# RWKV-7's running sums as TensorE products, and the experts' tokens and results as rows in DRAM placed by indirect transfers

## The chip, the cores and the metric

The kernel runs on one core of a Trainium2 chip. Such a core has TensorE (PE, matrix products), VectorE (DVE), ScalarE (ACT), GpSimd (POOL) and SyncE (SP, which here only issues transfers), each with a queue of its own that it works off in order, and 16 DMA engines. The metric is the device time of one execution in microseconds (us); lower is better.

## What is computed

The kernel computes two layers of a denoiser's backbone for 256 latent tokens and 256 context tokens of 1024 features, all in float32. Layer 0 is a bidirectional Mamba-2 mixer and a dense SwiGLU. Layer 1 is a bidirectional RWKV-7 mixer (called mixer 2 here, the second) and eight SwiGLU experts of 3584, of which each latent token uses two. The change touches layer 1:

```python
def _rwkv_features(u, ...):            # per direction d
    logw.append(_heads(-RW_DECAY_SCALE * jax.nn.sigmoid((w0[d] + jnp.tanh(xw @ w1[d]) @ w2[d]).astype(f32))))
    a = jax.nn.sigmoid((a0[d] + (xa @ a1[d]) @ a2[d]).astype(f32))
...
def _rwkv_scan(r, logw, k, v, kk, a, s0, need_y):
    ...
        sa = jnp.einsum('bhvk,bhk->bhv', S, kk_t)
        S = S * w_t[:, :, None, :] - sa[..., None] * b_t[:, :, None, :] + v_t[..., None] * k_t[:, :, None, :]
...
def _moe(u, router_w, w_in, w_out):
    logits = (u @ router_w).astype(jnp.float32)
    top_v, top_i = lax.top_k(logits, TOP_K)
    wts = jax.nn.softmax(top_v, axis=-1)
    gates = jnp.einsum('btk,btke->bte', wts, jax.nn.one_hot(top_i, N_EXPERTS, dtype=jnp.float32)).astype(u.dtype)
    for e in range(N_EXPERTS):
        out = out + gates[..., e:e + 1] * _swiglu(u, w_in[e], w_out[e])
```

## The kernel before

Every product with a weight matrix is made in three products of rounded float32 (`fp32r`): the operands are split in a high part (ACT's cast) and the rest (DVE's difference), and `mm3` adds hi·hi, hi·lo and lo·hi in PSUM (lines 212 to 214).

**Order.** The program is written as generators that `weave` interleaves; a scheduler then places each engine's instructions by a simulated timeline, and the engines work them off in that order. Buffers come from pools; a tile that takes over a buffer waits for the last use of the one before.

**Mixer 2** (924 to 1592 us of the profiled execution). The recurrence is worked in chunks of 64 tokens. Four units (context or latent tokens, first or second half of the heads) go through `stage`, once per direction. A direction of a unit has two pairs of chunks. `lora` makes, for a pair, the low-rank products and their sigmoids as Tanh: for each of four blocks of 128 features one product for the decay (L1013) and one for the rate (L1014), and a Tanh of 128x128 for each (L1015, L1017), with the bias `w0h` in the instruction; POOL adds 1 to the decays (`th`, L1023). `decays` runs once per chunk: a scan along the tokens on DVE (L1043, with `smask` zero where a block begins) gives the running sum `cum`, and ACT makes exp(−c·cum) (`Dp`, L1047), its last column (`dc`, L1049) and exp(c·cum) (L1050). `operands` scales by these, and `grams` makes the chunk's products (L1082, L1091). Between these run the inversions, the scans over chunks and the features of the other half, woven in.

**Experts** (1640 to 2641 us). Tokens lie in 128 slots per expert. `route(e)` makes one-hot matrices for a pair of experts (`one_hot`: DVE compares, PE transposes and a gate product) and `gather` multiplies the normalised tokens `uhi`/`ulo` by them (L1733, 32 products per pair), then scales, adds the modulation and splits into `xg`. `expert` goes over 28 tiles of the first matrix and 14 of the second, of 1 MB each, loaded by SP in that order (L1581) into 10 raw buffers; each is cast and differenced in two pieces (L1719, L1720, three buffers each) and used in 12 products. Seven times per expert the product of gate and value (L1754, L1756) is transposed (L1759) into `HT`. For each half of the output, DVE multiplies the result by gate and modulation (L1782), ACT and DVE split it (L1783, L1784), four products with the transposed one-hot send it back to its tokens (L1787, L1788), and DVE adds these to the residual (L1790). In experts 1, 3 and 5 `between` runs `route` for the next pair. Two lines set this:

```python
            nxt = (lambda: route(e + 1)) if e % 2 and e < 7 else None
            R = expert(so, PT[:, e % 2, :], gs[:, e % 2:e % 2 + 1], nxt, e == 7) or R
```

## Time and profile before

| what | before |
|---|---|
| median of three runs | 2652.65 us (2651.37 to 2655.88) |
| the profiled execution | 2658.37 us, its span 2656.5 us |
| mean granted clock of PE | 0.931 |
| PE, DVE, ACT, POOL busy | 92%, 77%, 55%, 13% of the span |
| layer 0: mixer, output product, dense SwiGLU | 0 to 924 us |
| mixer 2 | 924 to 1592 us |
| its end, routing | 1592 to 1640 us |
| the eight experts | 1640 to 2641 us |
| tail: final norm and output | to 2656.5 us |

The page's parts are averages over the span; the stages have different limits, so they are read stage by stage: the 40 slices for where a stage begins and ends, then the waits and the busy time in a stretch, then single lines. A wait is told as "engine, tile and line <- what ended it". The granted clock is that of PE, as a share of full speed (2.4 GHz; 0.5 is the lower of its two levels).

### The profile page before, as it was taken

To read this page: it belongs to the slowest core of one execution; us is meant where nothing else is said; L and a number is where in the kernel's file an instruction comes from. 1 tells how busy PE (TensorE), PEld (TensorE's weight loads), DVE (VectorE), ACT (ScalarE), POOL (GpSimd) and SP (SyncE) were. 2 spreads that over 40 slices of the span, in tenths; PEclk is the share of its full clock that TensorE was granted. 3 is DMA by queue.
4 is the path that set the end of the run, shared out by engine and by line. 5 is a ranking of instruction groups with operands and counts; after the bars stand their busy time and mean duration, and the time that the engine had idled before them with its cause. 6 is when DMAs were issued, how large, how long until landed. Compare 5 with 4: busy or idle time off the path is not lost. (4 is left out here: it accounts for less than half of the span.)

```text
span 2656.5 us, 44879 instructions
## 1 busy us (share of the span) xinstructions
PE 2440.9 (92%) x17770; PEld 1994.8 (75%) x17770; DVE 2039.1 (77%) x3070; ACT 1457.5 (55%) x2322; POOL 341.9 (13%) x434
## 2 busy tenths in 40 slices
PE   7999998999999978679868797999999999999997
PEld 4777776878888767568767686887888788878875
DVE  5787888667554377687676645999999899989997
ACT  4454545333223265435335225877787777778775
POOL 1011102000000254233432211000000000000001
PEclk9999999999999978577888687999999999999999
DMA  7323232336564221022020116899999899989994
GB/s 260 120 88 102 74 104 80 122 121 201 169 203 140 85 94 48 16 68 80 18 73 2 59 39 265 318 359 341 359 370 358 327 363 368 357 320 368 367 340 158
DMA packets 99211, 511.63 MB, mean 193 GB/s; under 512 B 11648, under 2 KB 19072, under 8 KB 55216
## 3 DMA queue, kind: packets, MB, share of 16 engines
q1 hardware_dynamic: 97520, 506.52, 52.8%
q8 instruction: 141, 2.31, 0.4%
q10 hardware_dynamic: 1472, 2.16, 0.3%
q14 instruction: 78, 0.64, 0.1%
HBM read 506.54 MB, written 2.10 MB: 191 GB/s over the span
## 5 line engine op out<-in xcount | busy, mean ns | idle before, releaser
L1720 DVE TENSOR_TENSOR wlo<-wraw,whi 128x1024 fp32r<-128x1024 f32 x662 | 798.4, 1224 | 69.6 <-ACT whi L1719 49.1
L1719 ACT CAST whi<-wraw 128x1024 fp32r<-128x1024 f32 x662 | 694.3, 1051 | 207.1 <-PE gu L214 111.9
L213 PE MATMUL gu<-wlo,xg 128*128 128x512 f32 x896 | 355.3, 397 | 1.5 <-DVE wlo L1720 0.7
L214 PE MATMUL gu<-whi,xg 128*128 128x512 f32 x896 | 349.8, 391 | 0.0
L212 PE MATMUL gu<-whi,xg 128*128 128x512 f32 x896 | 336.4, 392 | 1.1 <-ACT xg L1739 0.9
L206 ACT CAST whi<-wraw 128x1024 fp32r<-128x1024 f32 (+2 forms) x126 | 129.7, 1030 | 218.4 <-PE acc L213 206.2
L207 DVE TENSOR_TENSOR wlo<-wraw,whi 128x1024 fp32r<-128x1024 f32 (+2 forms) x126 | 151.8, 1205 | 110.0 <-ACT whi L206 109.8
L213 PEld LDWEIGHTS gu<-wlo,xg 128*128 128x128 f32 x896 | 168.5, 188 | 42.3 <-DVE wlo L1720 6.1
L212 PEld LDWEIGHTS gu<-whi,xg 128*128 128x128 f32 x896 | 168.4, 188 | 38.1 <-ACT xg L1739 1.6
L214 PEld LDWEIGHTS gu<-whi,xg 128*128 128x128 f32 x896 | 168.7, 188 | 31.5
L213 PE MATMUL y<-wlo,HT 128*128 128x512 f32 x448 | 178.4, 398 | 2.3 <-DVE wlo L1720 2.0
L212 PE MATMUL y<-whi,HT 128*128 128x512 f32 x448 | 176.6, 396 | 3.0 <-DVE xg L1740 3.0
L214 PE MATMUL y<-whi,HT 128*128 128x512 f32 x448 | 176.1, 393 | 0.0
L212 PE MATMUL acc<-h2hi,whi 128*128 128x512 f32 x352 | 137.4, 393 | 3.4 <-ACT h2hi L343 3.4
L1794 POOL TENSOR_TENSOR wraw<-yx,SH 128x512 f32<-128x512 f32 x4 | 7.5, 1875 | 1022.1 <-DVE yx L1790 1022.1
L213 PE MATMUL acc<-h2lo,whi 128*128 128x512 f32 x352 | 137.4, 391 | 0.0
L212 PE MATMUL acc<-hhi,whi 128*128 128x512 f32 (+1 forms) x328 | 135.8, 414 | 0.8 <-ACT whi L206 0.8
L214 PE MATMUL acc<-h2hi,wlo 128*128 128x512 f32 x352 | 134.7, 391 | 0.3 <-DVE wlo L207 0.3
L213 PE MATMUL acc<-hlo,whi 128*128 128x512 f32 (+1 forms) x328 | 134.1, 409 | 0.0
L214 PE MATMUL acc<-hhi,wlo 128*128 128x512 f32 (+1 forms) x328 | 133.6, 408 | 0.0
L305 POOL TENSOR_TENSOR sqa<-sqa,sq 128x512 f32<-128x512 f32 (+1 forms) x35 | 47.5, 1357 | 579.2 <-issue 311.3
L260 DVE SCALAR_TENSOR_TENSOR wraw<-wraw,scb 128x1024 f32<-128x1024 f32 x56 | 68.5, 1223 | 50.2 <-DMA wraw<-in_w_modT_dram 49.4
(565 smaller groups left out, 5358.5 us busy)
## 6 DMA issues: line engine op xcount, KB each, us to landing
wraw<-in_w_mi_dram SPq DMA_DIRECT2D x219, 1024.0 KB, 5.0
wraw<-in_w_mo_dram SPq DMA_DIRECT2D x112, 1024.0 KB, 5.0
wraw<-in_w_modT_dram SPq DMA_DIRECT2D x56, 512.0 KB, 3.9
wraw<-in_w_ffi_dram SPq DMA_DIRECT2D x44, 512.0 KB, 3.6
wraw<-in_w_mod_dram SPq DMA_DIRECT2D x40, 512.0 KB, 5.0
wraw<-in_w_mb_dram SPq DMA_DIRECT2D x40, 512.0 KB, 4.8
wraw<-in_w_mbo_dram SPq DMA_DIRECT2D x16, 512.0 KB, 4.1
wraw<-in_w_ffo_dram SPq DMA_DIRECT2D x16, 512.0 KB, 3.6
```

Of the source, the lines that this page charges most:

```text
L206: S.copy(hi, raw)
L207: eng[q % len(eng)].tensor_sub(lo, raw, hi.bitcast(F32))
L212: PE.matmul(o, whi, xhi, start=start, stop=False)
L213: PE.matmul(o, whi, xlo, start=False, stop=False)
L214: PE.matmul(o, wlo, xhi, start=False, stop=stop)
L260: V.scalar_tensor_tensor(t, w, 0.5, scb[:, j, :], op0=ALU.mult, op1=ALU.mult, accum_out=mods[l][:, n, j:j + 1])
L305: G.tensor_add(self.acc, self.acc, sq)
L1719: S.copy(hi, raw[:, k:k + 2, :])
L1720: V.tensor_sub(lo, raw[:, k:k + 2, :], hi.bitcast(F32))
L1794: G.tensor_mul(xf[:, tt, 512 * n:512 * n + 512], fs, fg[:, 512 * n:512 * n + 512])
```

## The change

**Mixer 2.** The biases `w0` and `a0` become a 65th row of the low-rank matrices, with a row of ones in the features, so that the Tanh needs no bias of its own: `th` is made with tokens on the partitions in one product of 512 columns and one Tanh, `ta` in four products and one Tanh. `decays` runs once per pair of chunks: four products of 128 columns with a triangular matrix of ones (`tb_f`, `tb_b`) give the running sum in PSUM, and ACT's exponentials read it there for both chunks at once. The second matrix is loaded in two transfers of 65 rows per unit.

**Experts.** Two tensors in DRAM, `XS` and `YS`, hold 128 rows for each expert and 128 more. They are filled with zeros where needed before the dense products of layer 0 (a memset and eight transfers of 0.5 MB on POOL's queue). The first pair is gathered as before. In expert 0 `slots` works out for every token the two rows it belongs to; POOL adds `uhi` and `ulo` and sends each token's row to both (four indirect transfers, 128 rows of 4 KB each). For the experts 2 to 7, SP loads the 128 rows of the expert and PE transposes them, 8 times 128x128, into the same scaling and split. The experts 0 to 6 multiply their result by the modulation alone and store it in `YS` from POOL's queue (14 transfers of 256 KB); in expert 7 `shares` gathers each token's two rows back (four indirect transfers) and DVE adds them with their weights. Expert 7 itself still goes back by its one-hot.

```diff
@@ lora, decays
-            th = tp.tile([128, 2, 4, 64], F32, name=f"th{d}")
+            th = tp.tile([128, 4, 128], F32, name=f"th{d}")
+            p = ms()
+            PE.matmul(p, F["hw"][d][:, ts], l2[0][:65, d], start=True, stop=True)
+            S.activation(flat(th), p, AF.Tanh, scale=0.5)
+            p = ms()
+            for i in range(4):
+                PE.matmul(p[:, 128 * i:128 * i + 128], l2[1][:65, d, 128 * i:128 * i + 128], F["ha"][d][:, ts],
+                          start=True, stop=True)
+            S.activation(flat(ta), p, AF.Tanh, scale=0.5)
             for i in range(4):
-                PE.matmul(p[:, 0:128], l2[:, 0, 128 * i:128 * i + 128], F["hw"][d][:, ts], start=True, stop=True)
-                PE.matmul(p[:, 128:256], l2[:, 1, 128 * i:128 * i + 128], F["ha"][d][:, ts], start=True, stop=True)
-                S.activation(th[:, :, i, :], p[:, 0:128].rearrange("p (c t) -> p c t", c=2), AF.Tanh,
-                             bias=w0h[:, 8 * d + k:8 * d + k + 1], scale=0.5)
-                S.activation(ta[:, i, :], p[:, 128:256], AF.Tanh, bias=w0h[:, 16 + 8 * d + k:17 + 8 * d + k], scale=0.5)
...
-        def decays(c):
-            V.tensor_tensor_scan(cum.rearrange("p k t -> p (k t)")[:, ::e], smask.rearrange("p k t -> p (k t)"),
-                                 th[:, c % 2].rearrange("p k t -> p (k t)")[:, ::e], 0.0, op0=ALU.mult, op1=ALU.add)
-            G.memset(Dp[:, :, 64 * d:64 * d + 1], 1.0)
-            S.activation(Dp[:, :, o:o + 64], cum, AF.Exp, scale=-0.3032655)
-            S.activation(un.dc[d][:, :, c:c + 1], cum[:, :, end:end + 1], AF.Exp, scale=-0.3032655)
-            S.activation(cum, cum, AF.Exp, scale=0.3032655)
+        def decays(pi):
+            for i in range(4):
+                PE.matmul(p[:, 128 * i:128 * i + 128], th[:, i, :], K2["tb_" + "fb"[d]], start=True, stop=True)
+            G.memset(Dp[:, :, :, 64 * d:64 * d + 1], 1.0)
+            S.activation(Dp[:, :, :, o:o + 64], cum, AF.Exp, scale=-0.3032655)
+            S.activation(un.dc[d][:, :, 2 * pi:2 * pi + 2], cum[:, :, :, 63 * o], AF.Exp, scale=-0.3032655)
+            S.activation(Di, cum, AF.Exp, scale=0.3032655)
...
@@ before the dense products
+        zt = fp.tile([128, D], F32, name="zt")
+        G.memset(zt, 0.0)
+        for i in range(2, 8):
+            G.dma_start(XS[128 * i:128 * i + 128], zt)
+        for i in (7, 8):
+            G.dma_start(YS[128 * i:128 * i + 128], zt)
...
@@ experts
+        def slots():
...
+            V.tensor_copy(ix, ef)
+            u = rows_tile()
+            for tt in range(2):
+                G.tensor_add(u[:, tt, :], uhi[:, tt, :].bitcast(F32), ulo[:, tt, :].bitcast(F32))
+                for r in range(2):
+                    G.indirect_dma_start(XS[:, :], bass.IndirectOffsetOnAxis(ap=ix[:, tt, r:r + 1], axis=0), u[:, tt, :], None)
+
+        def load_rows(e, t):
+            SY.dma_start(t[:, e % 2, :], XS[128 * e:128 * e + 128, :])
+            gather(128, 128 * (e % 2), lambda o, k: PE.transpose(o, t[:, e % 2, 128 * k:128 * k + 128], ident))
+
+        def shares():
+
+            for tt in range(2):
+                t = rows_tile()
+                for r in range(2):
+                    G.indirect_dma_start(t[:, r, :], None, YS[:, :], bass.IndirectOffsetOnAxis(ap=ix[:, tt, r:r + 1], axis=0))
+                for r in range(2):
+                    V.scalar_tensor_tensor(x3[:, tt, :], t[:, r, :], wt[:, tt, r:r + 1], x3[:, tt, :], op0=ALU.mult, op1=ALU.add)
...
+                if not last:
+                    yv = SH[:, 2 + n]
+                    V.tensor_mul(yv, o, m5r[:, 512 * n:512 * n + 512])
+                    G.dma_start(YS[128 * e:128 * e + 128, 512 * n:512 * n + 512], yv)
+                    continue
...
-        R = route(0)
-        for e in range(8):
-            PT, gs = R
-            so = 128 * (e % 2)
-            nxt = (lambda: route(e + 1)) if e % 2 and e < 7 else None
-            R = expert(so, PT[:, e % 2, :], gs[:, e % 2:e % 2 + 1], nxt, e == 7) or R
+        for e in range(7):
+            expert(128 * (e % 2), e, between=lambda: ahead(e))
+        _, PTe, gse = one_hot(7, 0)
+        expert(128, None, PTe, gse, shares)
```

**How the order moves.** ACT in the second half of the context's heads (1050 to 1122 us), in the first pair of chunks of both directions (0 and 1; `xu` is a PSUM bank): first the end of this as it stands before, then all of it as it stands in the changed kernel.

```order
L1015 ACTIVATE th_9117<-xu,w0h 128x2x64
L1017 ACTIVATE ta_9118<-xu,w0h 128x128
L1019 ACTIVATE kd_9110<-ta_9109,oka,ka_7477 128x128
L1019 ACTIVATE kd_9119<-ta_9118,oka,ka_7477 128x128
L1047 ACTIVATE Dp_9202<-cum_9200 128x4x64
L1049 ACTIVATE dc_9092<-cum_9200 128x4
L1047 ACTIVATE Dp_9228<-cum_9226 128x4x64
L1049 ACTIVATE dc_9092<-cum_9226 128x4
L1050 ACTIVATE cum_9200<-cum_9200 128x256
L1050 ACTIVATE cum_9226<-cum_9226 128x256
L1047 ACTIVATE Dp_9209<-cum_9207 128x4x64
L1049 ACTIVATE dc_9093<-cum_9207 128x4
```

```order
L1019 ACTIVATE th_9060<-xu 128x512
L1024 ACTIVATE ta_9061<-xu 128x512
L1029 ACTIVATE kd_9062<-ta_9061,oka,ka_7481 128x128 x4
L1019 ACTIVATE th_9072<-xu 128x512
L1024 ACTIVATE ta_9073<-xu 128x512
L1029 ACTIVATE kd_9074<-ta_9073,oka,ka_7481 128x128 x4
L1059 ACTIVATE Dp_9127<-xu 128x8x64
L1060 ACTIVATE dc_9042<-xu 128x4x2
L1062 ACTIVATE cum_9131<-xu 128x512
L1059 ACTIVATE Dp_9138<-xu 128x8x64
L1060 ACTIVATE dc_9043<-xu 128x4x2
L1062 ACTIVATE cum_9142<-xu 128x512
```

The pair now has four Tanh (of 512) where sixteen (of 128) stood, of which the last two stand at the head of the first list, and six exponentials where twelve stood; these read PSUM and no longer DVE's `cum`.

PE in expert 1, at the end of the gather for the next pair, before; then PE near the end of expert 1 in the changed kernel, where the rows of expert 3 (`YT`) are turned.

```order
L214 MATMUL gu_17994<-whi_18065,xg1_16290 128x512
L1733 MATMUL y_18154<-P_18092,uhi_15883 128x256 x2
L1733 MATMUL y_18154<-P_18092,ulo_15884 128x256 x2
L1733 MATMUL y_18141<-P_18092,uhi_15883 128x256 x2
L1733 MATMUL y_18141<-P_18092,ulo_15884 128x256 x2
L1759 MATMUL ms_18085<-cst_75,SH_16294 128x128 x4
L1733 MATMUL y_18154<-P_18092,uhi_15883 128x256 x2
L1733 MATMUL y_18154<-P_18092,ulo_15884 128x256 x2
L212 MATMUL y_18167<-whi_18168,HT0_16472 128x512
```

```order
L217 MATMUL y_18060<-whi_18083,HT0_16249 128x512
L1789 MATMUL y_18416<-cst_75,YT_17384 128x128
L218 MATMUL y_18060<-wlo_18084,HT0_16249 128x512
L219 MATMUL y_18060<-whi_18083,HT0_16249 128x512
L217 MATMUL y_18060<-whi_18083,HT0_16249 128x512
L218 MATMUL y_18060<-wlo_18084,HT0_16249 128x512
L219 MATMUL y_18060<-whi_18083,HT0_16249 128x512
L217 MATMUL y_18060<-whi_18087,HT0_16249 128x512
```

The block of 32 narrow products between the two matrices of an expert is gone; a transpose stands alone between the wide products of the second matrix, 12 or so of these apart.

SP in expert 0, where the loads of the second matrix are issued, before; then the same place in the changed kernel, and POOL's queue in the experts there (before, POOL had only L1794, four times, in this stage).

```order
L1581 DMA wraw_16998<-in_w_mo_dram 128x2048
L1581 DMA wraw_17020<-in_w_mo_dram 128x2048
L1581 DMA wraw_17042<-in_w_mo_dram 128x2048
L1581 DMA wraw_17075<-in_w_mo_dram 128x2048
L1581 DMA wraw_17097<-in_w_mo_dram 128x2048
L1581 DMA wraw_17119<-in_w_mo_dram 128x2048
L1581 DMA wraw_17141<-in_w_mo_dram 128x2048
```

```order
L1600 DMA wraw_16683<-in_w_mo_dram 128x2048
L1600 DMA wraw_16705<-in_w_mo_dram 128x2048
L1600 DMA wraw_16727<-in_w_mo_dram 128x2048
L1788 DMA YT_17384<-XS_4894 128x1024 x2
L1600 DMA wraw_16749<-in_w_mo_dram 128x2048
L1600 DMA wraw_16782<-in_w_mo_dram 128x2048
L1600 DMA wraw_16804<-in_w_mo_dram 128x2048
```

```order
L1783 TENSOR_TENSOR YT_16373<-uhi_15674,ulo_15675 128x1024 x2
L1785 DMA XS_4894<-YT_16373,ix_15682 1152x1024 x4
L1841 DMA YS_4895<-SH_16089 128x512 x14
L1796 DMA YT_23580<-YS_4895,ix_15682 128x1024 x2
L1796 DMA YT_23585<-YS_4895,ix_15682 128x1024 x2
L1858 TENSOR_TENSOR wraw_24083<-yx_12165,SH_16089 128x512 x4
```

The two loads of rows stand among the weight loads in SP's queue, and POOL issues four scatters, 14 stores and four gathers ahead of its last products.

## Rows read from the trace of the kernel before

**Rows 1.** The page's 40 slices of 66.4 us: PE busy, clock, GB/s.

```profile
PE   7999998999999978679868797999999999999997
...
PEclk9999999999999978577888687999999999999999
...
GB/s 260 120 88 102 74 104 80 122 121 201 169 203 140 85 94 48 16 68 80 18 73 2 59 39 265 318 359 341 359 370 358 327 363 368 357 320 368 367 340 158
```

**Rows 2.** Waits in 1640 to 2645 us, by total: us, times, longest us.

```profile
ACT whi L1719 <- PE gu L214: 115.9, 269, 3.2
...
PE ms L1759 <- DVE SH L1756: 4.6, 3, 1.5
...
DVE wlo L1720 <- DMA wraw<-in_w_mo_dram: 0.4, 1, 0.4
```

**Rows 3.** SP's own waits in the same stretch.

```profile
SPq L1581 <- DVE wlo L1720: 842.2, 320, 12.4
```

**Rows 4.** DVE's timeline, second halves' ends (experts 0, 1, 2, 6): start, us, instruction.

```profile
1767.61 0.75 DVE L1782 SCALAR_TENSOR_TENSOR SH<-y,gs,m5r 128x512 f32<-128x512 f32 x1
...
1894.95 0.74 DVE L1782 SCALAR_TENSOR_TENSOR SH<-y,gs,m5r 128x512 f32<-128x512 f32 x1
...
2015.85 0.74 DVE L1782 SCALAR_TENSOR_TENSOR SH<-y,gs,m5r 128x512 f32<-128x512 f32 x1
...
2515.67 0.75 DVE L1782 SCALAR_TENSOR_TENSOR SH<-y,gs,m5r 128x512 f32<-128x512 f32 x1
```

**Rows 5.** Three stretches: us, busy of PE, PEld, DVE, ACT, POOL, PEclk, DMA, GB/s.

```profile
1600.00:1630.00 30.00, 22.07 (x168) 20.97 (x168) 16.73 (x47) 15.72 (x31) 8.74 (x9) 0.84 1.01 419
1905.00:2005.00 100.00, 100.00 (x458) 82.59 (x457) 93.99 (x89) 79.95 (x85) 0.00 (x0) 1.00 0.97 367
2090.00:2110.00 20.00, 17.47 (x80) 14.23 (x79) 15.83 (x19) 13.93 (x19) 0.00 (x0) 0.91 0.69 249
```

**Rows 6.** The same view for two stretches of mixer 2.

```profile
985.00:1480.00 495.00, 391.37 (x6697) 343.25 (x6696) 354.04 (x759) 227.13 (x608) 180.01 (x259) 0.80 0.14 44
1050.00:1122.00 72.00, 43.77 (x1064) 38.30 (x1065) 50.90 (x131) 36.08 (x102) 17.54 (x33) 0.58 0.01 2
```

**Rows 7.** Waits in 985 to 1480 us.

```profile
POOL th L1023 <- ACT th L1015: 30.3, 7, 12.2
...
PE gr L1082 <- DVE BK L1061: 15.0, 2, 14.7
```

**Rows 8.** Groups by line, 1640 to 2645 us: busy us, mean ns | idle before.

```profile
L1754 ACT ACTIVATE SH<-gu 128x512 f32<-128x512 f32 x56 | 33.2, 593 | 0.9 <-PE gu L214 0.6
...
L1790 DVE TENSOR_TENSOR yx<-yx,sc 128x512 f32<-128x512 f32 x31 | 21.1, 680 | 0.6 <-PE sc L1788 0.6
L1787 PE MATMUL sc<-YT,PT 128*128 128x512 f32 x32 | 13.2, 412 | 2.3 <-ACT YT L1783 1.5 <-DVE yx L1790 0.8
...
L1706 PE MATMUL ms<-cst,P 128*128 128x128 f32 x12 | 2.3, 271 | 0.0
```

**Rows 9.** The page's DMA issues: count, KB each, median us to landing.

```profile
wraw<-in_w_mo_dram SPq DMA_DIRECT2D x112, 1024.0 KB, 5.0
...
wraw<-in_w_ffi_dram SPq DMA_DIRECT2D x44, 512.0 KB, 3.6
```

**Rows 10.** POOL's waits in 500 to 600 us.

```profile
POOL nt L335 <- DVE nh L342: 27.3, 1, 27.3
```

**Rows 11.** Groups by line in 985 to 1480 us.

```profile
L1043 DVE TENSOR_TENSOR_SCAN cum<-smask,th 128x256 f32<-128x256 f32 x32 | 25.0, 822 | 3.2 <-POOL th L1023 3.1
...
L1013 PE MATMUL xu<-hw,l 128*128 128x128 f32 x48 | 15.3, 413 | 1.8 <-ACT BT L1095 1.1 <-ACT ta L1017 0.7
...
L1047 ACT ACTIVATE Dp<-cum 128x256 f32<-128x256 f32 x32 | 13.3, 416 | 30.1 <-DVE cum L1043 29.5
...
L1015 ACT ACTIVATE th<-ms,w0h 128x128 f32<-128x128 f32 x32 | 11.9, 371 | 9.2 <-PE ms L1014 9.1
...
L1014 PE MATMUL ms<-ha,l 128*128 128x128 f32 x48 | 9.5, 281 | 0.0
```

More of the change, by code (lines that the diff above doesn't have):

```diff
@@ L1320, in tile_backbone @@
         F = {n: f0.tile([128, 8, 256], F32, name=n) for n in ("k", "kk")}
-        F.update({n: [f0.tile([128, 256], F32, name=f"{n}{d}") for d in range(2)] for n in ("hw", "ha")})
+        F.update({n: [f0.tile([65, 256], F32, name=f"{n}{d}") for d in range(2)] for n in ("hw", "ha")})
         for t in F["hw"] + F["ha"]:
-            G.memset(t, 0.0)
+            G.memset(t[64:], 1.0)
         rs = f0.tile([16, 256], F32, name="rs")
@@ L1535, in start_half @@
         later(hT, T["cs2"][:16, CS2["hselT"]:].rearrange("p (k f) -> p k f", k=8), after)
-        later(g2, T["w_l2"][:, 2, :], after)
+        later(g2, T["w_g2"], after)
         later(wr, T["w_rt"], after)
@@ L1564, in tile_backbone @@
     cnt = mo.tile([1, 8], I32, name="cnt")
+    wt = mo.tile([128, 2, 2], F32, name="wt")
+    oh2 = [mo.tile([128, 2, 8], F32, name=f"oh{r}") for r in range(2)]
+    ix = mo.tile([128, 2, 2], mybir.dt.uint32, name="ix")
     wmr = ctx.enter_context(tc.tile_pool(name="wmr", bufs=1, side="right", reuse_waits="tile"))
@@ L1723, in wsplit4, with gather @@
             return parts
-        def gather(ns, Pc):
+        def gather(ns, so, fill):
             n = 512 // ns
@@ L1738, in gather, with chosen, fill @@
                 pv = p.rearrange("p (k s) -> p k s", k=n)
-                S.copy(xg[0][:, k0:k0 + n, :ns], pv)
-                V.tensor_sub(xg[1][:, k0:k0 + n, :ns], pv, xg[0][:, k0:k0 + n, :ns].bitcast(F32))
-        def expert(so, PTe, gse, between=None, last=False):
+                hi, lo = (t[:, k0:k0 + n, so:so + ns] for t in xg)
+                S.copy(hi, pv)
+                V.tensor_sub(lo, pv, hi.bitcast(F32))
+        def chosen(Pc):
+            def fill(o, k):
+                for q, (src, tt) in enumerate(((uhi, 0), (uhi, 1), (ulo, 0), (ulo, 1))):
+                    PE.matmul(o, src[:, tt, 128 * k:128 * k + 128], Pc(tt), start=q == 0, stop=q == 3)
+            return fill
@@ L1745, in expert @@
+        def expert(so, e=None, PTe=None, gse=None, between=None):
+            last = e is None
             xhi, xlo = (lambda k, z=z: xg[z][:, k, so:so + 128] for z in range(2))
             for jc in range(7):
+                if jc == 2 and between:
+                    between()
                 o = [bank("gu", 4), bank("gu", 4)]
@@ L1764, in expert @@
                 V.tensor_sub(H[:, 1], p, H[:, 0].bitcast(F32))
-            nxt = between() if between else None
             if last:
@@ new lines, in columns, with one_hot @@
+        def columns(e, off, Pe):
+            for tt in range(2):
+                V.tensor_scalar(Pe[:, tt, :], C["iota"], float(off), rk[:, tt, e:e + 1], op0=ALU.add, op1=ALU.is_equal)
+        def one_hot(e, off):
+            Pe = mt.tile([128, 2, 256], F32R, name="P", bufs=1)[:, :, :128]
+            PTe = mt.tile([128, 256], F32R, name="PT", bufs=1)
+            gse = mt.tile([128, 1], F32, name="gs", bufs=1)
+            columns(e, off, Pe)
+            p = misc()
+            for tt in range(2):
+                PE.transpose(p[:, 128 * tt:128 * tt + 128], Pe[:, tt, :].bitcast(F32), ident)
+            S.copy(PTe, p[:, :256])
+            p = misc()
+            for tt in range(2):
+                PE.matmul(p[:, :1], Pe[:, tt, :].bitcast(F32), gate[:, tt, e:e + 1], start=tt == 0, stop=tt == 1)
+            V.tensor_copy(gse, p[:, :1])
+            return Pe, PTe, gse
@@ new lines, in tile_backbone, with ahead @@
+        P = mt.tile([128, 2, 256], F32R, name="P", bufs=1)
+        for e in range(2):
+            columns(e, 0, P[:, :, 128 * e:128 * e + 128])
+        gather(256, 0, chosen(lambda tt: P[:, tt, :]))
+        pair = []
+        def ahead(e):
+            if e == 0:
+                slots()
+                return
+            if e % 2:
+                pair[:] = [rows_tile()]
+            load_rows(e + 1, pair[0])
+        for e in range(7):
+            expert(128 * (e % 2), e, between=lambda: ahead(e))
```

134 lines of the change are left out of this document (66 added, 68 removed).

## The prediction, made before the changed kernel had run

> **What bounds the kernel now.** I read the 40 slices of the page first, since the change touches two stages that have different limits. In the granted-clock row the last 15 slices (the experts, from about 1660 us) stand at nine tenths or more, and PE with them in all but the last, while the slices of mixer 2 (the 15th to the 24th, 924 to 1592 us) show PE at six to nine tenths, a clock of 0.5 to 0.8 and under 100 GB/s of DMA [rows 1].
>
> Experts: next I read the waits of that stage. ACT's cast of the weights waits for PE (115.9 us by the product of the first matrix); PE itself waits 4.6 us in all for its largest reason; and DVE waits once, for 0.4 us, for a load [rows 2]. SP waits 842 us for a buffer to come free, over 320 loads [rows 3]. So PE is the bound and every other engine follows it, the loads included. How long an expert takes I read from the end of its second half, where L1782 runs once: 1767.61, 1894.95, 2015.85 us for experts 0 to 2 [rows 4]. Expert 1 took 127.34 us and expert 2 took 120.90. The one gathers the next pair's tokens in it, the other does not. In a clean stretch PE is busy for the whole of 100 us at clock 1.00 (458 matmuls, 0.218 us each); over a gather, 2090 to 2110, it is busy for 17.47 of 20, the clock falls to 0.91 and the loads from 367 to 249 GB/s [rows 5].
>
> Mixer 2: over 985 to 1480 us, PE is busy 79%, DVE 72%, ACT 46%, POOL 36%, at clock 0.80 [rows 6]. No engine is full: part is bound by PE's slow products, part by chains from engine to engine. 1050 to 1122 is the plainest chain: PE 43.77 of 72 us, clock 0.58 [rows 6], with one wait of 14.7 us on DVE's operand [rows 7].
>
> **The change, experts.** Per pair the gather by one-hot products goes for three of the four pairs. Its price with everything behind it (the two one-hots, the waits, the clock) is the surplus of the pitches: from expert 0's end to expert 6's, 2515.67 − 1767.61 = 748.06 us; six clean pitches are 6 × 120.90 = 725.4; so three gathers cost 22.7 us [rows 4]. In their place come 8 transposes per expert, set one at a time between wide products; and out of each of the experts 0 to 6 go the 8 scatter products. A scatter product shows 412 ns of modelled time, a transpose 271 [rows 8], and PE's real pace is 0.218 us an instruction; at that pace eight out and eight in are 1.75 us each and cancel. Bounds for a transpose: 0.11 us (its 128 columns are a quarter of 512) to 0.27, so −0.9 to +0.4 us per expert. I take −0.3, near the pace. Expert 6 has no transposes but expert 7's one-hot (4 short instructions): −0.9. Expert 0 loses 8 one-hot instructions, and scatters against transposes: −1.75. Expert 7 keeps its scatter. Sum: −22.7 − 5 × 0.3 − 0.9 − 1.75 = **−27 us**.
>
> DVE and ACT in this stage only follow. Per expert DVE loses four adds of 680 ns [rows 8] and two differences of the same 128x512, and gains two such differences and four scalings of a quarter of the width: about 2 us less than in a clean expert. The four multiply-adds of 128x1024 in expert 7 (twice an add's width, 1.4 us each) come to 5.5 us there. ACT trades two casts for two. I put these at nothing; the cover is that both wait for PE now, and without it expert 7 would pay the 5.5.
>
> DMA: each of the experts 2 to 7 loads 0.52 MB of token rows, experts 0 to 6 write 0.52 MB of results, expert 0 writes 2.1 MB (every token twice) and expert 7 reads 2.1 MB: 11 MB more. A clean expert needs 42 × 1.05 + 1.05 = 45.1 MB in 120.6 us (120.90 − 0.3), 374 GB/s, against 367 seen there and 419 with the queue deep at 1600 to 1630 [rows 5]. The 367 is what PE asked for, since SP waited for buffers, not a limit; so I put the bytes at nothing, and keep the other end as a rival. The Trainium skill ("DMA: Bandwidth & Descriptors", Where 436 GB/s comes from) speaks against this: it gives some 358 GB/s for a core's HBM traffic and 435 for the fabric. The rows pass the first figure (367 in the steady stretch, 419 in the burst), so the trace does not agree with it for a core alone.
>
> New waits. In expert 0, at its 13th weight tile of 42, DVE has the row numbers ready; POOL adds two halves and issues four indirect transfers, one after the other. SP's first load of rows stands after the 33rd weight load of that stretch, with all later weight loads behind it, and is reached about the 23rd tile. A tile is 120.9 / 42 = 2.88 us, so there are 29 us before SP stands, and 10 buffers of 2.88 us less the 5.0 us of a landing [rows 9] and the split, some 20 us, before PE starves: 49 us for four transfers of 0.5 MB. A plain 0.5 MB transfer lands in 3.6 us [rows 9]. No row shows an indirect transfer or one from POOL's queue, so its price lies between 3.6 us and unknown; below 12 us nothing is late. In expert 7 the four reads of result rows stand behind the last store of expert 6 (tile 1 of expert 7); DVE wants the first two at tile 20 (50 us) and the second two, which wait for the buffer of the first, some 10 tiles later (27 us). I put both at nothing. The stores of results take the buffer that DVE's next product (tiles 4 and 8 of the next expert) overwrites; three tiles, 8.6 us, cover it.
>
> The zero fill (a memset, eight 0.5 MB transfers on POOL's queue) stands ahead of POOL's first multiply of the norm before the dense products, before which POOL idles 27.3 us [rows 10]; eight issues fit unless each takes 3 us. Nothing.
>
> **The change, mixer 2.** Out: 32 scans of 0.82 us on DVE (25 us); 128 Tanh of 0.37 us on ACT (four groups like the one shown, 47 us), against 32 of 128x512, by the SiLU of that size 0.59 us (19 us); 64 Exp of 0.41 (26 us), against 32 of double width, by the same 0.6 (19 us) [rows 8, 11]. ACT: −35 us; DVE: −25. In: 64 products of 128 columns on PE, 18 us by the 281 ns of the same size in one bank's group and 26 by the 413 ns of the other's [rows 11]. Four tanh products become one of 512 columns (16 times): the same columns, so nothing to 3 us less. So two lighter engines against 15 to 26 us of PE.
>
> What lies on the path? Where the chain sets the end, each of 8 phases (both directions side by side) saves 12 of 16 Tanh in a row, 3.5 us, and the scan gives way to four products of about the same length; POOL's add, which waits 30.3 us for the Tanh [rows 7], starts earlier, and the next thing late is POOL's own multiplies. Two or three of the stages are like that (1050 to 1122 above all): −12 to −20 us. Where PE is the bound (the other five phases), 5 × 2 × 4 × 0.28 = 11 us come on, less 2 for the wider product. I take −15 + 9 = **−6 us**; ends −25 (all chains, products in PE's gaps) and +20 (all products on the path, nothing saved).
>
> **Sum.** The profiled execution took 2658.37 us, 5.7 above the median of 2652.65. 2658.4 − 27 − 6 = 2625.4; against the median, **2620 us**.
>
> **The rivals.** (a) The DMA is the bound after all. At 367 GB/s, six pitches with 271 MB need 738 us against 723 of PE; 15 us, and 11 more for the ends in experts 0 and 7, less some of the 20 us of buffers: about 17 of the gain lost, 2637. For: the DMA's share there is already 0.97 [rows 5]. Against: landings stay at 5.0 us and SP waits for buffers. By the Trainium skill's 358 GB/s the 271 MB take 757 us, 19 more, and nothing would be left of the gain.
>
> (b) Slower: the indirect transfers are slow, and SP's queue, in order, holds the weights behind them. With s us each, PE loses 4s − 49 in expert 0 and 2s − 27 at the second reads of expert 7. At s = 18 this is 23 + 9 = 32 us, the whole gain; at s = 22, 39 + 17 = 56, 2676 us. It decides from 18 us, five times a plain landing. For: POOL issues them while DVE is 94% busy [rows 5], and no row has a price. Against: a row of tokens is 4 KB in one piece, and POOL has nothing else to do in this stage. The Trainium skill ("SBUF — State Buffer", Who interferes with whom) has a mechanism: descriptors that POOL writes starve while DVE is in a two-port mode, though by it a tensor_tensor has none; no row here shows either.
>
> (c) The products of the running sum land on the path: +20 in mixer 2, so 2652.65 − 27 + 20 = 2646 us. For: PE is at nine tenths in two slices of that stage; against: ACT and DVE are waited for as well.
>
> (d) The chains were the bound nearly everywhere: −25 in mixer 2, 2601 us.
>
> **How the numbers follow.** Forecast 0.52 (2608 to 2632 with the bounds of the transposes and half of mixer 2's), (a) 0.13, (b) 0.13, (c) 0.10, (d) 0.12. What a measurement of this kernel can tell from no change is about 0.2%, 5 us. Slower: (b) less its mild cases, 0.12. Same: the edge of (b) and (c), 0.06. Faster: 0.82. The range leaves out (b) and the edges of (c) and (d): 2594 to 2650.
>
> **What would show it.** Experts: the ends of the second halves 120 to 121 us apart throughout, no dip of the DMA row between experts, the row loads without a wait on SP. (a) shows as DVE waiting for loads and landings above 6 us; (b) as SP waiting for POOL's transfers in expert 0 or DVE for them in expert 7, PE idle. Mixer 2: 924 to 1592 us becomes about 662, with ACT's waits for the scan gone; (c) shows as PE busy longer there by 18 us or more with the stage no shorter. Wrong altogether would be a gap of PE at the transposes, each of which stands in PE's order between wide products and so holds them if its rows are late.

## The result and the profile after

The changed kernel takes 2635.23 us in the median of five executions (2625.79 to 2636.51), against 2652.65 before; the ratio is 0.9937, with a 95% interval of 0.9912 to 0.9961. That is 17 us gained where the forecast was 33: the sign and the range held, and about half of the gain is missing. Where it came from is not where the forecast had it.

The profiled execution has a span of 2634.6 us, 21.9 less than before. Three anchors divide it: the first `mx` of mixer 2 on DVE (933.67 us before, 937.52 after), ACT's last `rv`, which ends mixer 2 (1599.56 and 1583.74), and the end of the last expert's second half (2640.81 and 2618.94).

| stretch | before | after | difference | forecast |
|---|---|---|---|---|
| to the first features of mixer 2 (with the zero fill) | 933.7 | 937.5 | +3.9 | 0 |
| mixer 2 | 665.9 | 646.2 | −19.7 | −6 |
| routing and experts | 1041.3 | 1035.2 | −6.1 | −27 |

**Experts.** DVE's timeline at the ends of the second halves (L1840, in the place of L1782 in [rows 4]), experts 0 to 2 and 6:

```profile
1752.58 0.68 DVE L1840 TENSOR_TENSOR SH<-y,m5r 128x512 f32<-128x512 f32 x1
...
1872.66 0.68 DVE L1840 TENSOR_TENSOR SH<-y,m5r 128x512 f32<-128x512 f32 x1
...
1998.99 0.68 DVE L1840 TENSOR_TENSOR SH<-y,m5r 128x512 f32<-128x512 f32 x1
...
2490.64 0.68 DVE L1840 TENSOR_TENSOR SH<-y,m5r 128x512 f32<-128x512 f32 x1
```

Expert 1 took 120.1 us, as it should without a gather. Expert 2 took 126.3, and the six together 738.1, against 748.06 before and 723 forecast; expert 7, outside the six, took 128.3 against 125.1 before. Something other than the gather costs time now, from expert 2 on. It is in the waits of 1640 to 2645 us (us in all, times, longest), to be read against [rows 2]:

```profile
ACT whi L1728 <- PE gu L219: 103.7, 278, 2.3
...
ACT HT L1824 <- PE ms L1820: 33.9, 30, 2.6
...
POOL XS L1785 <- DMA XS<-YT,ix: 19.4, 3, 8.5
...
DVE wlo L1729 <- DMA wraw<-in_w_mi_dram: 0.9, 3, 0.4
```

ACT's cast of the transposed product (`HT`) waits for PE's transposes 33.9 us. Before, in the same stretch, that wait was:

```profile
ACT HT L1763 <- PE ms L1759: 10.0, 10, 1.0
```

DVE waits for loads 0.9 us in all, so the 11 MB more cost next to nothing. The new transfers, from the DMA issues of 1640 to 2645 us (count, KB each, median us to landing):

```profile
wraw<-in_w_mi_dram SPq DMA_DIRECT2D x207, 1024.0 KB, 6.1
...
YS<-SH POOLq DMA_DIRECT2D x14, 256.0 KB, 5.9
...
XS<-YT,ix POOLq DMA_INDIRECT x4, 8.4
YT<-YS,ix POOLq DMA_INDIRECT x4, 7.7
```

What the wait on PE does is seen in ACT's timeline, in expert 1 and then at the start of expert 2 (what ended the idle time before stands in brackets):

```profile
1790.14 0.58 ACT L1824 CAST HT<-ms 128x512 fp32r<-128x512 f32 x1
1801.54 0.58 ACT L1824 CAST HT<-ms 128x512 fp32r<-128x512 f32 x1
1812.90 0.58 ACT L1824 CAST HT<-ms 128x512 fp32r<-128x512 f32 x1
...
1903.38 0.58 ACT L1824 CAST HT<-ms 128x512 fp32r<-128x512 f32 x1 [2.57 <-PE ms L1820]
1914.03 0.59 ACT L1824 CAST HT<-ms 128x512 fp32r<-128x512 f32 x1 [0.97 <-PE ms L1820]
1925.81 0.59 ACT L1824 CAST HT<-ms 128x512 fp32r<-128x512 f32 x1 [0.97 <-PE ms L1820]
```

Two things are new. A block of four weight tiles mostly takes 11.38 us in the experts 0 and 1 and 11.79 from expert 2 on: `HT` now stands in ACT's order half a tile earlier against PE, so ACT waits 0.97 us in each, and the weight casts behind it come later. And at 1903.38 (again at 2152.03) the wait is 2.57 us, and PE runs dry behind it, first for ACT's cast and then for DVE's difference:

```profile
1904.97 0.50 PE L217 MATMUL gu<-whi,xg 128*128 128x512 f32 x1 [1.62 <-ACT whi L1728]
1906.22 0.53 PE L218 MATMUL gu<-wlo,xg 128*128 128x512 f32 x1 [0.76 <-DVE wlo L1729]
```

DVE's timeline says why. In expert 1 the product of gate and value (L1817) stands behind three differences in a row; here it stands behind five, and the next casts and differences follow that much later:

```profile
1783.77 3.65 DVE L1729 TENSOR_TENSOR wlo<-wraw,whi 128x1024 fp32r<-128x1024 f32 x3 [0.20 <-ACT whi L1728]
1787.33 0.68 DVE L1817 TENSOR_TENSOR SH<-SH,gu 128x512 f32<-128x512 f32 x1
...
1894.50 6.67 DVE L1729 TENSOR_TENSOR wlo<-wraw,whi 128x1024 fp32r<-128x1024 f32 x5 [0.33 <-ACT whi L1728]
1901.09 0.68 DVE L1817 TENSOR_TENSOR SH<-SH,gu 128x512 f32<-128x512 f32 x1
```

The buffer it writes is shared with the result that is being stored (L1841), for which it must wait by its order. Whether that sets its place is for an experiment.

**Mixer 2.** The waits and groups in 985 to 1480 us, to be read against [rows 7, 11]. First the waits:

```profile
POOL th L1034 <- ACT th L1019: 50.4, 10, 14.7
```

then the groups (busy us, mean ns, idle before):

```profile
L1055 PE MATMUL xu<-c,th 128*128 128x128 f32 x64 | 14.0, 392 | 0.0
...
L1055 PE MATMUL ms<-c,th 128*128 128x128 f32 x64 | 10.3, 307 | 0.0
...
L1059 ACT ACTIVATE Dp<-ms 128x512 f32<-128x512 f32 x8 | 4.8, 596 | 4.8 <-PE ms L1055 4.8
L1059 ACT ACTIVATE Dp<-xu 128x512 f32<-128x512 f32 x8 | 4.8, 596 | 6.3 <-PE xu L1055 6.2
L1019 ACT ACTIVATE th<-ms 128x512 f32<-128x512 f32 x8 | 4.8, 595 | 5.2 <-PE ms L1018 5.2
```

The sums cost PE 24 us of busy time, inside the forecast's 18 to 26, and ACT's new Tanh and exponentials take 0.6 us as estimated. ACT's 29.5 us of waits for the scan are gone; 11 for the sums' products came (4.8 and 6.2, before `Dp`). POOL's wait for the Tanh didn't shrink, it grew from 30.3 to 50.4 us. The stretch as a whole, from its first features to its last `rv`, before and after (columns as in [rows 5]):

```profile
933.67:1599.56 665.89, 531.42 (x8552) 465.33 (x8552) 462.50 (x1032) 290.73 (x757) 227.12 (x311) 0.78 0.15 51
```

```profile
937.52:1583.74 646.22, 541.05 (x8584) 465.18 (x8584) 441.01 (x1004) 264.58 (x614) 218.13 (x294) 0.80 0.17 55
```

PE is busy 10 us more and idle 29 us less (134.5 to 105.2); its granted clock is 0.80 in place of 0.78.

**The fill.** POOL's timeline: the eight issues cost 4.45 us, and POOL still idles 26.6 us before the norm, as forecast. But DVE's timeline shows a load of modulation weights that came late behind the 4.2 MB:

```profile
534.12 3.40 POOL L656 DMA_DIRECT2D XS<-zt  x6 [0.31 <-POOL zt L654]
537.51 1.05 POOL L658 DMA_DIRECT2D YS<-zt  x2
...
565.21 2.81 POOL L340 TENSOR_TENSOR nt<-X,rbx 128x512 f32<-128x512 f32 x1 [26.64 <-DVE nh L347]
```

```profile
548.42 1.22 DVE L265 SCALAR_TENSOR_TENSOR mprod<-wraw,scb 128x1024 f32<-128x1024 f32 x1 [6.39 <-DMA wraw<-in_w_modT_dram]
```

### The profile page after: what moved, and what is told of

Read it like the earlier page. It is cut to its first block, busy times and chain, and to the rows that moved or that the text cites. A ratio compares the mean times of both kernels' runs of the same rounds, so it can differ in the third digit from the quotient of the medians.

```text
span 2634.6 us, 44522 instructions
## 1 busy us (share of the span) xinstructions
PE 2439.1 (93%) x17658; PEld 1967.3 (75%) x17658; DVE 2001.2 (76%) x3011; ACT 1424.6 (54%) x2169; POOL 362.2 (14%) x449
## 5 line engine op out<-in xcount | busy, mean ns | idle before, releaser
L218 PE MATMUL gu<-wlo,xg 128*128 128x512 f32 x896 | 362.7, 405 | 8.9 <-DVE wlo L1729 5.6
L217 PE MATMUL gu<-whi,xg 128*128 128x512 f32 x896 | 348.5, 394 | 4.8 <-ACT whi L1728 3.5
L219 PE MATMUL gu<-whi,xg 128*128 128x512 f32 x896 | 351.6, 393 | 0.0
L1841 POOL DMA_DIRECT2D YS<-SH x14 | 7.6, 546 | 789.0 <-DVE SH L1840 789.0
L786 POOL TENSOR_TENSOR wlo<-wraw,whi 128x512 fp32r<-128x512 f32 (+1 forms) x69 | 87.0, 1268 | 146.3 <-ACT whi L785 118.6
## 6 DMA issues: line engine op xcount, KB each, us to landing
wraw<-in_w_mi_dram SPq DMA_DIRECT2D x219, 1024.0 KB, 6.1
wraw<-in_w_mo_dram SPq DMA_DIRECT2D x112, 1024.0 KB, 5.3
```

The source lines that it names most:

```text
L217: PE.matmul(o, whi, xhi, start=start, stop=False)
L218: PE.matmul(o, whi, xlo, start=False, stop=False)
L219: PE.matmul(o, wlo, xhi, start=False, stop=stop)
L786: self.eng[self.n % len(self.eng)].tensor_sub(lo, raw, hi.bitcast(F32))
L1841: G.dma_start(YS[128 * e:128 * e + 128, 512 * n:512 * n + 512], yv)
```

## The experiments

Theory after the traces: (E) in the experts the gather's price is gone, and two new costs ate most of it, the shared buffer and the order from expert 2 on; (M) mixer 2 gains because the scan is gone from DVE and from the chain that the others wait for; (F) the fill costs some 4 us by its traffic. The rivals stand with each run. Each ratio is to the kernel before on the same chip; times from different chips are a few us apart for one kernel, so the ratios are what is compared. "Mixer 2" below is the time between the first two anchors, as in the table: with the old code it is 659.4 to 667.3 us (three profiles), with the new one 641.5 to 646.6 (nine).

**One half of the change alone.** The kernel before with the new experts and the fill, and the kernel before with the new mixer 2:

```diff
@@ experts only, against before (lora and decays untouched)
-            gather(256, lambda tt: P[:, tt, :])
...
+                    G.dma_start(YS[128 * e:128 * e + 128, 512 * n:512 * n + 512], yv)
...
+        for e in range(7):
+            expert(128 * (e % 2), e, between=lambda: ahead(e))
@@ mixer 2 only, against before (route, gather and expert untouched, no fill)
-        def decays(c):
+        def decays(pi):
...
+                PE.matmul(p[:, 128 * i:128 * i + 128], th[:, i, :], K2["tb_" + "fb"[d]], start=True, stop=True)
```

> Mixer 2 as before, the experts by rows in DRAM and the zero fill as in the changed kernel. By the prediction's terms (experts -27, fill 0) this is 27 us faster than before. By the reading of the two traces the experts give 4 to 7 us and the fill takes 4 to 5 back, since a modulation load lands 6 us late behind it: within 5 us of before, pitches of 126, 122, 126, 122, 122 us for experts 2 to 6.

> Mixer 2 as in the changed kernel, the experts as before and no zero fill. By the prediction's term this is 6 us faster than before; by the reading of the two traces about 20 us faster, with the whole gain between 985 and 1500 us and the experts at their old pitches of 127, 121, 129, 121, 130, 120 us.

The experts alone: 2649.11 us, ratio 0.9985 (0.9969 to 1.0001); the six pitches sum to 738.1 us as in the changed kernel, and the features start at 937.24. Mixer 2 alone: 2633.14 us, 0.9931 (0.9911 to 0.9951), mixer 2 in 645.2 us, the old pitches (the first 1.6 us longer, the others within 0.2). So the halves hardly touch each other, and nearly the whole gain is mixer 2's: the division by anchors holds.

**A buffer of its own for the stored result.**

```diff
-                    yv = SH[:, 2 + n]
+                    yv = mt.tile([128, 512], F32, name="yv", bufs=1)
```

> The changed kernel, but the result that an expert stores has a buffer of its own, so the next expert's product of gate and value no longer shares it. Theory (order): in experts 2 and 4 the second block's product was placed two tiles late because of the store, which costs a pause of PE of 2.4 us and a dip of the clock; gone, experts 2 and 4 take 122 us as 3 and 5 do: 7 us faster than the changed kernel. Rival (traffic): the added bytes slow the loads and with them DVE; bytes are the same here, so 0 us.

2622.5 us, ratio 0.989 (0.9866 to 0.9914). From the last `rv` to the last half's end it took 1023.95 us in place of 1035.2: 11.2 us, more than the 7 expected, with the same bytes, so the rival falls. DVE's product of gate and value in the second block of expert 2, at 1901.09 in the changed kernel, moved forward:

```profile
1889.27 1.23 DVE L1729 TENSOR_TENSOR wlo<-wraw,whi 128x1024 fp32r<-128x1024 f32 x1 [0.33 <-ACT whi L1728]
1890.41 0.68 DVE L1817 TENSOR_TENSOR SH<-SH,gu 128x512 f32<-128x512 f32 x1
```

The pitches of the experts 2 to 6 lie between 121.2 and 121.9 (that of expert 1 holds the end of the half, which moved), PE's gaps at the start of the experts 2 and 4 are gone, but the 0.97 us waits stay:

```profile
ACT HT L1824 <- PE ms L1820: 32.9, 35, 1.0
```

So the shared buffer cost some 11 us (over all profiles, seven with the shared buffer took 1032.1 to 1036.0 us and the two with an own one 1024.0 and 1024.4, so 8 to 12), and the longer blocks are another matter.

**`HT`'s cast later in ACT's order.** On top of the own buffer, the cast was tied to a later weight cast by a small instruction on ACT:

```diff
-                S.copy(H[:, 0], p)
-                V.tensor_sub(H[:, 1], p, H[:, 0].bitcast(F32))
+                def split(w, H=H, p=p):
+                    one = mt.tile([128, 1], F32, name="one", bufs=2)
+                    S.activation(one, w[:, 0:1].bitcast(F32), AF.Identity, scale=0.0, bias=C["ones"][:, :1])
+                    S.activation(H[:, 0], p, AF.Identity, scale=one[:, 0:1])
+                    V.tensor_sub(H[:, 1], p, H[:, 0].bitcast(F32))
+                pend.append(split)
```

> As e3_own_buffer, and ACT's cast of the transposed product is tied to a later cast of weights, so that in ACT's order it stands 3 tiles behind its block, where before it stood 2.5 and in the changed kernel from expert 2 on 2. Theory (order): ACT then no longer waits 0.97 us per block for PE's transposes, a block takes 11.4 us in place of 11.8, experts 2 to 7 lose 2.9 us each: 17 us faster than e3_own_buffer, some 24 faster than the changed kernel. Rival (traffic): 0 us, and DVE starts to wait for loads.

A miss: 2636.68 us, ratio 0.9938 (0.9917 to 0.996), 14 us slower than with the own buffer alone. ACT no longer waits for the transposes, but PE waits for the differences, and a block takes 12.2 us:

```profile
PE gu L218 <- DVE wlo L1729: 20.8, 37, 1.4
```

The scheduler set the SiLU and `HT` next to each other, behind eight weight casts, so the weights came later still. The old order was not restored, and ACT's own work grew: the small instruction takes 0.29 us and the cast in this form 0.68 in place of 0.58, 0.4 us per block. So this run says only that taking the wait away is not enough; it doesn't part the wait from the place in the order.

**The gather taken out of the kernel before.** The three later gathers are left out and nothing put in their place; the experts 2 to 7 then work on the first pair's tokens.

```diff
-            gather(256, lambda tt: P[:, tt, :])
+            if e == 0:
+                gather(256, lambda tt: P[:, tt, :])
```

> The kernel before without the three later gathers: experts 2 to 7 work on the first pair's tokens, scatter and all else stay. Theory (phase): without a gather's pause the scheduler's order for ACT drifts, from expert 3 on, by one cast to the order that the changed kernel has from expert 2 on, and a block of the first matrix takes 11.8 us in place of 11.4: pitches of 121 for experts 1 and 2, 122 for 3 and 123 to 124 for 4 to 6, 13 to 15 us faster than before. Rival (the prediction's term): all pitches 120 to 121, 22.7 us faster.

2638.15 us, ratio 0.9961 (0.9943 to 0.9979). The six pitches sum to 734.9 us: 13.2 less than 748.06, not 22.7. No row load, store or shared buffer is in this kernel, and yet the wait comes, from the fourth block of expert 3 on:

```profile
2044.70 0.58 ACT L1763 CAST HT<-ms 128x512 fp32r<-128x512 f32 x1
2056.02 0.59 ACT L1763 CAST HT<-ms 128x512 fp32r<-128x512 f32 x1 [0.98 <-PE ms L1759]
2067.81 0.59 ACT L1763 CAST HT<-ms 128x512 fp32r<-128x512 f32 x1 [0.98 <-PE ms L1759]
```

with the block going from 11.38 to 11.79 us there. So the gather's surplus was not all price. In the kernel before, all seven blocks of expert 7 have it already (11.79 us, seven of the ten waits) and the other experts don't; without gathers it sets in at expert 3, and 9.5 of the 22.7 us don't come. Not all of that is the longer blocks: the one-hot matrices of the three later pairs are still made here, as they are not in the changed kernel, and expert 1, without one longer block, took 121.5 us against 120.09 of expert 2. By estimate 25 blocks at 0.41 us make 10 us and three pairs of one-hots some 4; that is more than 9.5 because a clean pitch is 120.1 here and not the 120.9 of the prediction. Why the scheduler's order slips by half a tile, and whether it can be held, stays open.

**The fill moved** behind the norm, into the dense products:

```diff
-        zt = fp.tile([128, D], F32, name="zt")
...
         ft = es.enter_context(tc.tile_pool(name="ft", bufs=2, reuse_waits="tile"))
+        zt = ft.tile([128, D], F32, name="zt", bufs=1)
+        G.memset(zt, 0.0)
```

> The changed kernel with the zero fill moved behind the norm, into the dense products. Theory (queue): the fill's 4.2 MB held up a modulation load that DVE stands on, 6.4 us, and with it the norm; moved, that wait is gone: 4 to 5 us faster than the changed kernel. Rival (the prediction's term): the fill costs nothing where it is, 0 us.

2627.47 us, ratio 0.991 (0.9891 to 0.9929), an interval that overlaps that of the changed kernel. The features of mixer 2 start at 930.56 in place of 937.52. DVE's waits for those weights in 525 to 600 us, here, in the changed kernel and before:

```profile
DVE mprod L265 <- DMA wraw<-in_w_modT_dram: 8.0, 5, 3.9
DVE mprod L265 <- DMA wraw<-in_w_modT_dram: 16.2, 6, 6.4
DVE mprod L260 <- DMA wraw<-in_w_modT_dram: 11.2, 6, 4.2
```

Over the profiles, mixer 2 starts at 932.7 to 938.4 us in the eight profiles with the early fill (mean 936.1) and at 928.7 to 933.7 in the four without one (mean 931.4): the fill costs some 5 us.

**Both mended**, the own buffer and the later fill:

> The changed kernel with both mends, the stored result's own buffer and the fill behind the norm. If the two gains add: 4 to 5 us faster than e3_own_buffer's 2622.5, about 2618.

2615.75 us, ratio 0.988 (0.9861 to 0.9899): the fastest of all, and 15 us below the changed kernel by the ratios. The two gains add, as expected.

**What mixer 2 gained by.** Four runs take one candidate each. Every product of the running sum made twice; the 128 Tanh back at 128x128; the scan's cost put back by two scans per direction and pair, over `th` in place (by minimum and maximum, which leave it as it is), with PE's products behind them; and, in the kernel before, the scans kept but the exponentials of two chunks made at once.

```diff
@@ sums twice, against the changed kernel
-                PE.matmul(p[:, 128 * i:128 * i + 128], th[:, i, :], K2["tb_" + "fb"[d]], start=True, stop=True)
+                for _ in range(2):
+                    PE.matmul(p[:, 128 * i:128 * i + 128], th[:, i, :], K2["tb_" + "fb"[d]], start=True, stop=True)
@@ Tanh in four, against the changed kernel (and so for ta)
-            S.activation(flat(th), p, AF.Tanh, scale=0.5)
+            for i in range(4):
+                S.activation(th[:, i, :], p[:, 128 * i:128 * i + 128], AF.Tanh, scale=0.5)
@@ scan kept, against the changed kernel
+            for z in range(2):
+                t = flat(th)[:, 256 * z:256 * z + 256]
+                V.tensor_tensor_scan(t, t, t, 0.0, op0=ALU.min, op1=ALU.max)
@@ by pairs, against before
-        def decays(c):
+        def decays(pi):
...
+            cum = tp.tile([128, 2, 4, 64], F32, name=f"cum{d}")
...
+            for z in range(2):
+                V.tensor_tensor_scan(cum[:, z].rearrange("p k t -> p (k t)")[:, ::e], smask.rearrange("p k t -> p (k t)"),
+                                     th[:, z].rearrange("p k t -> p (k t)")[:, ::e], 0.0, op0=ALU.mult, op1=ALU.add)
...
+            S.activation(Dp[:, :, :, o:o + 64], cum, AF.Exp, scale=-0.3032655)
```

> The changed kernel with each of the 64 products of the running sum made twice (the second overwrites the first with the same numbers). Theory (gaps): PE has room in mixer 2, the products lie beside chains of other engines: at most 5 us slower than the changed kernel. Rival (path, the prediction's term): the products stand on the path in five of eight phases, 11 us slower, and 18 to 26 if in all.

> The changed kernel with each Tanh of 128x512 made in four of 128x128, 128 in all as before the change, 28 us more of ACT; the running sum stays on PE. If the shorter row of Tanh is what mixer 2 gained by: 12 to 20 us slower than the changed kernel. If the gain is in the scan's going (DVE, and one pair of exponentials for two chunks): at most 5 us slower.

> The changed kernel itself on the chip of the run beside it, for the comparison: 0.9937 of before, about 2634 us.

> The kernel before, with only one thing of the change: the scans, the 128 Tanh and everything else stay, but the running sums of a pair's two chunks are made one behind the other and their exponentials for both at once (16 pairs of exponentials of 128x512 where 32 of 128x256 stood). Mixer 2 took 665.9 us before, from its first features to its last normalisation, and 643 to 647 in the kernels with the change. Theory (the scan's going is what shortens it): 658 to 668, time within 0.3% of the kernel before. Rival (what counts is that the decays of two chunks are made together, once per pair): 643 to 652, 14 to 22 us faster than before. Second rival (PE's clock and order in the features of the latent tokens, 92 us before and 84 after, in a stretch that holds none of the changed instructions): 650 to 660, with that stretch alone at 84 to 86.

> The changed kernel with the scan's cost put back: behind POOL's addition of 1, DVE runs two scans of 128x256 over th in place (by minimum and maximum, which leave th as it is), 32 in all, 0.82 us each or 26 us, and TensorE's products wait for them. So each pair's chain is 1.6 us longer than in the changed kernel and as long as a scan made it before. Theory (the scan's going is what shortens mixer 2): 656 to 668 us from the first features to the last normalisation, most of the 20 us lost again. Rival (decays made once per pair): 643 to 650, the scans hidden. Second rival (order and clock): between, 648 to 658, with the features of the latent tokens still at 84 to 86 us.

| kernel | us | ratio (95%) | mixer 2 | PE idle in it | clock in it |
|---|---|---|---|---|---|
| before | 2652.65 | | 665.9 | 134.5 | 0.78 |
| changed | 2635.23 | 0.9937 (0.9912 to 0.9961) | 646.2 | 105.2 | 0.80 |
| changed, run again | 2630.76 | 0.9926 (0.9909 to 0.9943) | 643.1 | 106.6 | 0.80 |
| sums twice | 2632.52 | 0.9949 (0.9931 to 0.9967) | 645.9 | 101.2 | 0.82 |
| Tanh in four | 2631.53 | 0.9925 (0.9909 to 0.9941) | 646.4 | 102.6 | 0.79 |
| scan kept | 2637.35 | 0.9961 (0.9944 to 0.9977) | 646.3 | 111.2 | 0.81 |
| before, by pairs | 2648.01 | 0.9998 (0.9974 to 1.0023) | 656.3 | 138.4 | 0.80 |

*The products.* Doubling them made mixer 2 no longer, so the rival of 11 us or more falls. That they lie in PE's gaps doesn't follow: they cost PE 38.8 us in place of 24.3, and its idle time fell by 4 only. The rest of PE's work went faster, at a granted clock of 0.82 in place of 0.80:

```profile
936.17:1582.07 645.90, 544.71 (x8712) 471.22 (x8712) 438.85 (x1004) 264.51 (x613) 220.18 (x294) 0.82 0.17 55
```

*The Tanh.* The run with four short ones is as fast as the changed kernel, so their number isn't what counts. Their time isn't tested by it, since it didn't come back:

```profile
L1020 ACT ACTIVATE th<-ms 128x128 f32<-128x128 f32 x32 | 6.3, 284 | 5.0 <-PE ms L1018 4.9
```

The same group took ACT 11.9 us before [rows 11]; over the four groups it is 25.7 us here, 19.1 in the changed kernel and 47.3 before, so 7 of the expected 28 us were put back.

*The scan.* The theory of the scan falls as the main cause: with 22 us of scans back on DVE and PE waiting for them, mixer 2 stays at 646.3.

```profile
L1039 DVE TENSOR_TENSOR_SCAN th<-th 128x256 f32<-128x256 f32 x32 | 22.3, 736 | 15.0 <-POOL th L1034 15.0
...
L1058 PE MATMUL xu<-c,th 128*128 128x128 f32 x64 | 14.8, 402 | 4.7 <-DVE th L1039 4.7
```

That profile was of the fastest of its eight executions; by the ratios the scan costs 6 to 9 us (the interval lies just apart from that of the changed kernel run again and overlaps that of its first run), PE's idle time 6 of 29.

*Pairs, and the clock.* Pairs alone show no gain in time; their 656.3 us is 3 us below the lowest other profile of old code, and inside the 650 to 660 of that run's second rival. It spoke of the features of the latent tokens, which hold none of the changed instructions but one small memset on POOL. Here they are taken from DVE's first `mx` for these tokens to PE's last product with it (columns as in [rows 5]): before, by pairs, changed.

```profile
1165.46:1278.54 113.08, 100.82 (x1084) 89.63 (x1086) 84.72 (x155) 57.32 (x131) 48.18 (x47) 0.76 0.27 85
```

```profile
1166.17:1270.20 104.03, 90.47 (x1084) 81.11 (x1086) 84.97 (x155) 56.92 (x129) 48.01 (x47) 0.87 0.29 92
```

```profile
1164.41:1269.12 104.71, 94.30 (x1084) 84.39 (x1086) 83.57 (x155) 57.45 (x129) 47.78 (x46) 0.82 0.29 92
```

PE runs 1084 instructions each time, and the stretch is 8 to 9 us shorter, at a granted clock of 0.87 and 0.82 in place of 0.76. The other two profiles of old code show 114.0 and 113.6 us at 0.76; the others with the new one lie between 103.9 and 105.6, except 109.8 with the sums twice. So some 8 to 9 of the 20 us stand in a stretch of which the change leaves the work alone; they came with the clock, and in the profile of pairs alone too. Over the ten executions of that kernel they don't show: those lie between 2634.0 and 2658.0 us, at mean clocks of 0.928 to 0.939, and the profiled one had 0.938. Why the clock is higher there is not shown.

The other 10 us or so are open. The scan has a part; the time of the Tanh, and the low-rank products in two PSUM banks per pair, where four stood, with the biases inside them, were not undone by any run. Mixer 2's gain is measured (17 us by the medians of the run with mixer 2 alone), the cause of its greater part is not.

## Why the prediction was half right

- **The price of the gather, −22.7 us: a step that failed.** It compared pitches with and without a gather and took the difference as what goes. It held for expert 1 (120.1 us). Leaving the gathers out gave 13.2, mostly because the order drifts without them; a pitch is the product of an order, and the order is remade. The blocks of expert 7, longer already in the trace of before, were the sign of it, and I didn't look at them.
- **"The stores ... three tiles, 8.6 us, cover it": failed.** The store lands in 5.9 us, and no instruction waited for it in the trace. The cost came through the place that the scheduler gave the product: some 11 us, by the run with the own buffer, of a shortfall of 21 (27 − 6). In that run 1041.25 us became 1023.95, so 17.3 of the 27 came; of the 9.7 that are missing the longer blocks are the largest part seen (five pitches of 121.2 to 121.9 against 120.1, 8 us), and POOL's adds in expert 0 took 3.6 (last section); a clean pitch of 120.1, shorter than the 120.6 reckoned with, gives some back.
- **Transposes: right in size.** A transpose shows 271 ns, as before, and no gap of PE stands at one.
- **DMA at nothing, rival (a): right.** The six pitches came to 738.1 us, the very sum of rival (a), by chance: DVE waited 0.9 us for loads, and with the same bytes the own buffer took 11 us off. One of its two signs came, as the first matrix's loads landed in 6.1 us in the median, where they had landed in 4.9. The engines moved 405 GB/s over 1700 to 1760 us and 376 over 1760 to 1870. The Trainium skill ("DMA: Bandwidth & Descriptors", Where 436 GB/s comes from) gives some 358 GB/s as what binds transfers from HBM to SBUF; the trace does not agree with that for a core alone.
- **Indirect transfers, put at nothing against rival (b): right.** 8.4 and 7.7 us in the median and 11.0 at most, below the 12 from which something is late; SP waited 5.8 us for them once, and DVE's 0.9 us of waits say that this stayed within its cover.
- **The zero fill at nothing: failed, some 5 us.** I costed the issues on POOL and not the traffic ahead of a load for which DVE stood already (4.2 us at the longest before).
- **Mixer 2, −15 + 9 = −6: the size failed, and neither reason is borne out.** The +9 for products on the path did not show (sums twice, though at a higher clock). The −15 was for chains in two or three stages; 8 to 9 of the −20 came in the features of the latent tokens, for which the prediction had no term, with PE's clock, and what the shorter Tanh saved no run shows. −20 lies inside the bounds I gave (−25 to +20), near rival (d). The mechanism that would have told me so was not found.
- **64 products at 18 to 26 us: a wrong reading that came out right.** The trace holds two records for each of these products (64 in each of the two groups, 128 in all), and the mean of a record counts time in which records overlap. By busy time [rows 11] gives 0.40 to 0.64 us a product, 25 to 41 us in all; measured are 0.38 and 24.

The total came out in the range because misses of opposite sign met: experts 21 us short, mixer 2 14 us better, the fill 4 worse. That is luck, not working.

## What to carry to other kernels

A surplus between two stretches of a scheduled kernel is not the price of the work that lies in one of them: take the work out, alone, before its price is put in a sum. Where a transfer gets a buffer that an engine on the critical path also writes, cost the place in the order and not only the wait, and give it a buffer of its own if there is room. A transfer that nobody waits for can still delay the one that somebody stands on. And before a stage's gain is put down to the edit, look at a stretch of it that the edit leaves alone, and at the clock there.

## What the runs showed of the hardware

POOL's four scatters of 128 rows of 4 KB land in 8.4 us in the median (4.3 to 10.1) and the gathers in 7.7 (6.4 to 11.0), the scatters beside loads, with 340 GB/s in all over 1670 to 1705 us; a plain 256 KB store from POOL's queue lands in 5.9 (5.2 to 7.7). In this program each scatter is issued when the one before has landed (POOL's waits for that come to 19.4 us).

While POOL adds two tiles of 128x1024 (1664.36 to 1670.1 us), DVE's differences of the same size take longer, and PE runs dry twice behind them (POOL, DVE, PE):

```profile
1664.36 5.74 POOL L1783 TENSOR_TENSOR YT<-uhi,ulo 128x1024 f32<-128x1024 f32 x2 [62.15 <-DVE ix L1780]
```

```profile
1664.87 6.31 DVE L1729 TENSOR_TENSOR wlo<-HT,whi 128x1024 fp32r<-128x1024 f32 x2
1671.10 1.21 DVE L1729 TENSOR_TENSOR wlo<-wraw,whi 128x1024 fp32r<-128x1024 f32 x1
```

```profile
1667.90 0.50 PE L218 MATMUL gu<-wlo,xg 128*128 128x512 f32 x1 [1.22 <-DVE wlo L1729]
1671.24 0.49 PE L218 MATMUL gu<-wlo,xg 128*128 128x512 f32 x1 [1.45 <-DVE wlo L1729]
```

Two take 6.31 us in place of 2.4, PE stands for 2.7 us behind them, and the block of four weight tiles there takes 15.0 us in place of 11.4. The prediction had no term for it. The Trainium skill ("SBUF — State Buffer", Who interferes with whom) says that a DVE instruction with two inputs in SBUF contends with a POOL instruction that reads SBUF; the trace agrees. My prediction named that section for POOL's descriptors and passed over this sentence of it.
